# A pool-mixer trunk on one core: three products of its second input phase as seven inner products in place, the output weights formed and split only behind them

## The chip, the cores and the metric

The kernel runs on one core of one Trainium2 chip. The metric is the device time of one execution in microseconds (us); smaller is better. Executions of this kernel before the change took 909.81 to 910.54 us.

## The reference

With DEPTH = 1 only the pooling mixer runs: a row norm, an input projection to 2 x 1024 channels (values `u` and a gate), trailing means over 2, 4, 8 or 16 frames minus the value itself in four groups of 256 channels, a 256 x 256 map for each group, bias, scale, SiLU gate, an output projection, the residual sum and a last row norm. x is 4096 rows of 1024 float32.

```python
normed = rms_norm(h, norm_w[i])
u, gate = jnp.split(normed @ in_w, 2, axis=-1)
ug = u.reshape(b, s, POOL_GROUPS, POOL_GROUP_DIM)
pooled = jnp.stack([trailing_mean(ug[:, :, g], w) for g, w in enumerate(POOL_WINDOWS)], axis=2) - ug
mixed = jnp.einsum('bsgc,gcd->bsgd', pooled, group_w) + group_b
y = mixed.reshape(b, s, POOL_WIDTH) * scale * jax.nn.silu(gate)
h = h + y @ out_w
return rms_norm(h, final_norm_w)
```

## The kernel before, in words

The group maps are folded into the value half of the input weights at the start. All large products are then done by Winograd's form of Strassen's scheme: a product of 2 x 2 blocks in seven block products P1 to P7 with sums and differences around them. Every operand is split into two float32r parts (`split`: ScalarE copies the high part, VectorE subtracts it from the operand for the low part), and a block product is three passes of matmuls (`mm3`, L603).

Three phases follow each other in the list `steps`: "a" and "b" (the first and the second half of the input projection's columns, NB = 4 blocks of 1024 rows each) and "o" (the output projection, 8 blocks of 512 rows). A step is one block product. In "a" and "b" the order is `ORDER_IN` = P1, P2, P7, P6, P5, P4, P3, and a step is 48 matmuls of 128x512 (`product_in`): four PSUM banks, in each two halves h of the contraction, two k, three passes. P1, P2, P7, P4 use banks 0 to 3 ("x" and "v"), P6, P5, P3 banks 4 to 7 ("y"), into which P1 is copied first (`evict_in`). P5 is added onto y after P6 has been copied out of it. In the later steps of phase "o", one P2 product is itself done with seven inner products (`product_inner`, L701), of 128x256 matmuls.

What lies around a step: `advance("load", ...)` loads operands three steps ahead, `advance("split", ...)` splits the operand of the next step into the four tiles `ops`, two of them for a step, `form(n + 2)` forms the sums two steps ahead, `pool_due` issues the pooling of an earlier block half, `run(n)` the product and its eviction. Behind `run`, `make_wo` (at P5 of blocks 1 and 2 of phase "b") loads a quarter pair of the output weights, scales it in place (`scale_rows`, L246), forms Winograd's sums (`combine`, four VectorE instructions of 128x1024) and stores them to the DRAM tiles `wod`; in block 3, `load_w` (after every step) loads one product's weights from `wod` and splits them into `w`.

SBUF tiles of 4 KB a partition come from two lists, `st` (NS = 11) and `vt` (NV = 8). `take` hands out the tile that was given back longest ago; whoever writes it waits for its last users, a DMA store included.

The order of the instructions on each engine is fixed when the kernel is built: the framework plays the program through with its own durations and lets each engine take, of what is ready, what the program names first. So an instruction can stand ahead of others that the program names before it, when those were not ready. `tc.issue_after(x)` keeps the instructions of its block, where they are on the engine of x, behind x.

Of the kernel before, what the change touches and what calls it, by code (L numbers as in the profile page):

```python
# [15 lines left out]
P = 128  # L16
# [48 lines left out]
def kernel(  # L65
# [54 lines left out]

    def renew(t):
        i = next(i for i, u in enumerate(sts) if u is t)
        return mem.tile([P, D], F32R, tag=f"st{i}", name=f"inner{i}")

    st.renew = renew
    vt = Slots(
        [mem.tile([P, 2 * (HIST + H)], F32, tag=f"vt{i}", name=f"vt{i}") for i in range(NV)]
    )
# [23 lines left out]
    def give(ap):  # L152
        next(p for p in (st, vt, early, early5) if id(ap) in p.used).give(ap)
# [343 lines left out]


    xs = [{} for _ in range(NB)]
    turn = [0]  # L500

    def next_op(pattern, **sizes):
        t = ops[turn[0] % 4]
        turn[0] += 1
        return t.rearrange(pattern, **sizes)

    first_saves = []

    def split_halves(us, saved=None):
        ts = []  # L510
        for h, u in enumerate(us):
            t = next_op("p (s a b) -> p s a b", s=2, a=2)
            split(t, u)
# [33 lines left out]
    def form_in(q, b, i):  # L547

        s = xs[b]
        if i in (P1, P2):  # L550
            if q == 0:
                for u in s["11" if i == P1 else "12"]:
                    normalize(b, 0, u)
        elif i == P7:
            if q == 0:
                for h in range(2):
                    normalize(b, 1, s["21"][h])
                    sub(s["21"][h], s["11"][h], s["21"][h])
        elif i == P6:
            s["2"] = [take(pool=early if (q, b) == (0, 0) else None) for _ in range(2)]  # L560
            for h in range(2):
                if q == 0:
                    normalize(b, 1, s["22"][h])
                sub(s["2"][h], s["22"][h], s["21"][h])
            for u in s.pop("21"):
                give(u)
            if q == 0:
                give(rstd.pop(b))
        elif i == P5:
            for h in range(2):  # L570
                add(s["11"][h], s["2"][h], s["11"][h])
            if (q, b) != (0, 0):
                for u in s.pop("2"):
                    give(u)

    def split_in(q, b, i):
        s = xs[b]
        key = {P1: "11", P2: "12", P6: "2", P7: "21", P5: "11", P4: "22", P3: "12"}[i]
# [11 lines left out]
    stores = []  # L590

    def form_s4(b):
        for u, s2 in zip(xs[b]["12"], xs[b]["2"]):
# [49 lines left out]
    def form_inner(stage):  # L643
# [13 lines left out]
                give(u)  # L657
            return
        r = inner_w["sums"][stage - 1]
        hi, lo = (kept.pop().rearrange(pattern, **sizes) for _ in range(2))  # L660
        copy(hi, r)
        sub(lo, r, hi.bitcast(F32))
        give(r)
# [480 lines left out]
    def run(n, between=None, behind=None, seeds=4):  # L1144
        kind, b, i = steps[n]
        sets = sets_of(kind, b)
        if kind == "o":
            product_out(i, split_up.pop(n), sets, n == len(steps) - 1)
            evict_o(b, i, sets)
        else:  # L1150
            product_in(i, split_up.pop(n), sets, i == P1, between, behind)
            evict_in(b, 0 if kind == "a" else 1, i, sets, seeds)

    pending = []

    def pool_later(n):
        kind, b, i = steps[n]
# [202 lines left out]

    scales, summed = {}, []
    stages = (P6, P5, P4)
    stages = (P6, P5, P4)

    for n in range(2, len(steps)):
        kind, b, i = steps[n]
# [55 lines left out]
        if kind in ("a", "b"):  # L1422
            pool_later(n)
            if kind == "a":
                pool_due(n)
            if kind == "b" and b == NB - 1:
                load_w(wod, i)
            if kind == "b" and b in (1, 2) and i == P5:
                make_wo(b - 1)
            if kind == "b" and b == NB - 1 and i == P3:  # L1430
                f = take("p (a b) -> p a b", a=2)
                nc.sync.dma_start(
                    out=f.rearrange("p a b -> p (a b)"), in_=final_w.partition_broadcast(P)
                )
                fw.append(f)
# [52 lines left out]
```

## Time and profile before

| | |
|---|---|
| median of 3 executions | 910.12 us (909.81 to 910.54) |
| profiled execution: time, span | 910.49 us, 908.7 us |
| granted TensorE clock | 0.999 |
| TensorE busy | 900.7 us, 99% of the span, 4320 matmuls |
| VectorE, ScalarE, GpSimd busy | 715.5, 485.9, 84.6 us |
| steps of phase "b", block 1: P1, P2, P7, P6, P5 begin at about | 397, 407.5, 417.9, 428.2, 438.6 us |

A step is 10.36 us long. The profile gives, for a group of instructions, the line, the engine, output<-input tiles, the shape, the count, then busy us and the mean ns of one, then the idle time of the engine ahead of them and what ended it. The difference of 1.8 us between time and span lies outside the span and is taken as unchanged.

### The profile page before, as it was taken

To read this page: it belongs to the slowest core of one execution; us is meant where nothing else is said; L and a number is where in the kernel's file an instruction comes from. 1 tells how busy PE (TensorE), PEld (TensorE's weight loads), DVE (VectorE), ACT (ScalarE), POOL (GpSimd) and SP (SyncE) were. 2 spreads that over 40 slices of the span, in tenths; PEclk is the share of its full clock that TensorE was granted. 3 is DMA by queue.
4 is the path that set the end of the run, shared out by engine and by line. 5 is a ranking of instruction groups with operands and counts; after the bars stand their busy time and mean duration, and the time that the engine had idled before them with its cause. 6 is when DMAs were issued, how large, how long until landed. Compare 5 with 4: busy or idle time off the path is not lost.

```text
span 908.7 us, 11590 instructions
## 1 busy us (share of the span) xinstructions
PE 900.7 (99%) x4320; PEld 790.1 (87%) x4320; DVE 715.5 (79%) x843; ACT 485.9 (53%) x735; POOL 84.6 (9%) x166
## 2 busy tenths in 40 slices
PE   9999999999999999999999999999999999999997
PEld 7888888888888888888888888888888898988886
DVE  3889995985995997685786599599759768868686
ACT  7869547447446555355345445645545535445444
POOL 0020100100110000000000000001122113212200
PEclk9999999999999999999999999999999999999999
DMA  9987776577575454134616715618585675675732
GB/s 343 401 300 230 268 241 240 190 267 245 218 271 193 162 207 140 47 140 138 255 72 217 267 70 174 200 54 225 179 234 160 169 205 162 163 220 156 180 139 94
DMA packets 70841, 178.10 MB, mean 196 GB/s; under 512 B 6528, under 2 KB 24320, under 8 KB 70784
## 3 DMA queue, kind: packets, MB, share of 16 engines
q1 hardware_dynamic: 58160, 144.82, 46.0%
q0 software_dynamic: 11904, 31.48, 13.3%
q10 hardware_dynamic: 720, 1.06, 0.3%
q8 instruction: 34, 0.56, 0.3%
q14 instruction: 23, 0.19, 0.1%
HBM read 116.50 MB, written 60.83 MB: 195 GB/s over the span
## 4 chain that ended last, share of the span: by engine, by line
PE 95%; DVE 2%; DMA 1%; ACT 1%; issue 0%; DVEq 0%; ACTq 0%; SPq 0%
PE bank L603 89%; PE bank L701 3%; PE bank L406 3%; DMA st<-wvd 1%; DMA t3d<-st 0%; DMA early<-in_group_w 0%; DVE vt L1067 0%; DVE st L159 0%; ACT st L974 0%; ACT st L446 0%; DVE vt L162 0%; PE bank L472 0%; DVE op L159 0%; DVE vt L1026 0%; DVE st L156 0%
## 5 line engine op out<-in xcount | busy, mean ns | idle before, releaser
L603 PE MATMUL bank<-op,w 128*128 128x512 f32 x2688 | 581.2, 379 | 0.2 <-ACT st L165 0.2
L603 PEld LDWEIGHTS bank<-op,w 128*128 128x128 f32 x2688 | 507.8, 189 | 72.9 <-ACT st L165 0.6
L603 PE MATMUL bank<-w,op 128*128 128x512 f32 (+1 forms) x1212 | 262.2, 377 | 0.0
L603 PEld LDWEIGHTS bank<-w,op 128*128 128x128 f32 x1212 | 226.0, 189 | 31.0
L159 DVE TENSOR_TENSOR op<-st,op 128x1024 fp32r<-128x1024 f32 x129 | 156.5, 1220 | 76.4 <-ACT op L165 76.0
L165 ACT ACTIVATE op<-st 128x1024 fp32r<-128x1024 f32 x129 | 134.7, 1052 | 123.3 <-PE bank L603 82.6
L165 ACT ACTIVATE vt<-bank 128x512 f32<-128x512 f32 x105 | 61.4, 593 | 44.7 <-PE bank L603 44.2
L159 DVE TENSOR_TENSOR op<-vt,op 128x1024 fp32r<-128x1024 f32 x43 | 52.4, 1220 | 20.8 <-ACT op L165 20.6
L165 ACT ACTIVATE op<-vt 128x1024 fp32r<-128x1024 f32 x43 | 45.0, 1052 | 28.9 <-PE bank L603 24.9
L165 ACT ACTIVATE st<-bank 128x512 f32<-128x512 f32 x67 | 39.0, 592 | 38.0 <-PE bank L603 26.1
L884 POOL DMA_DIRECT2D st<-in_x x19 | 16.9, 894 | 387.7 <-DVE op L159 354.1
L159 DVE TENSOR_TENSOR st<-st,st 128x1024 f32<-128x1024 f32 (+1 forms) x43 | 46.7, 1108 | 3.2 <-ACT st L943 1.3
L165 ACT ACTIVATE bank<-bank 128x512 f32<-128x512 f32 x48 | 27.9, 581 | 35.6 <-PE bank L603 35.4
L755 DVE TENSOR_TENSOR_SCAN vt<-vt,window 128x1040 f32<-128x1040 f32 x16 | 38.1, 2379 | 2.8 <-ACT vt L165 2.7
L159 DVE TENSOR_TENSOR w<-st,w 128x1024 fp32r<-128x1024 f32 x25 | 30.2, 1220 | 11.7 <-ACT w L165 11.7
L165 ACT ACTIVATE w<-st 128x1024 fp32r<-128x1024 f32 x25 | 26.0, 1052 | 16.3 <-PE bank L603 10.8
L806 DVE SCALAR_TENSOR_TENSOR st<-vt,colt,st 128x512 f32<-128x512 f32 x46 | 32.4, 746 | 1.7 <-ACT st L165 1.6
L165 ACT ACTIVATE st<-st 128x1024 f32<-128x1024 f32 x16 | 16.9, 1058 | 29.9 <-DVE st L156 29.7
L801 DVE SCALAR_TENSOR_TENSOR vt<-vt,vt 128x1024 f32<-128x1024 f32 x24 | 29.3, 1221 | 0.3
L947 DVE SCALAR_TENSOR_TENSOR vt<-vt,ors,st 128x1024 f32<-128x1024 f32 x18 | 22.5, 1282 | 8.0 <-POOL ors L225 8.0
L162 DVE TENSOR_TENSOR st<-st,vt 128x1024 f32<-128x1024 f32 x22 | 26.1, 1216 | 2.1 <-DMA vt<-rd 2.1
L1067 DVE TENSOR_TENSOR st<-bank,st 128x512 f32<-128x512 f32 x23 | 15.8, 689 | 13.8 <-PE bank L603 13.7
(136 smaller groups left out, 661.6 us busy)
## 6 DMA issues: line engine op xcount, KB each, us to landing
st<-in_xt SPq DMA_DIRECT2D x28, 512.0 KB, 5.9
sd<-st POOLq DMA_DIRECT2D x28, 512.0 KB, 4.3
st<-sd SPq DMA_DIRECT2D x24, 512.0 KB, 4.4
yd<-st SPq DMA_DIRECT2D x23, 512.0 KB, 2.6
st<-in_x SPq DMA_DIRECT2D x20, 512.0 KB, 6.3
st<-yd SPq DMA_DIRECT2D x20, 512.0 KB, 4.7
out<-vt SPq DMA_DIRECT2D x18, 512.0 KB, 4.5
st<-wod SPq DMA_DIRECT2D x15, 512.0 KB, 3.4
```

The source lines that it names most:

```text
L159: return nc.vector.tensor_tensor(out=dst, in0=a, in1=b, op=ALU.subtract)
L162: nc.vector.tensor_tensor(out=dst, in0=a, in1=b, op=ALU.mult)
L165: return nc.scalar.activation(dst, src, func)
L406: latest[0] = nc.tensor.matmul(ps, a[:, kk, 2 * j + t, :], maps, start=t + m == 0, stop=t == 1 and m == len(pairs) - 1,).ins
L603: latest[0] = nc.tensor.matmul(ps, a, b, start=start and n == 0, stop=stop and n == 2, skip_group_check=True).ins
L701: latest[0] = nc.tensor.matmul(ps, x1, x2, start=i in (P1, P7) and k + n == 0, stop=k == 1 and n == 2, skip_group_check=True,).ins
L755: nc.vector.tensor_tensor_scan(out=sums_[:, HIST:], data0=flat[:, HIST:], data1=flat[:, HIST - win : 2 * end - win], initial=first_sum, op ...
L801: nc.vector.scalar_tensor_tensor(out=s[:, :, at : at + H], in0=s[:, :, at : at + H], scalar=1.0 / win, in1=v[:, :, HIST:], op0=ALU.mult, o ...
L806: nc.vector.scalar_tensor_tensor(out=sg[:, j], in0=s[:, j, at : at + H], scalar=bias_c[2 * grp + j], in1=sg[:, j], op0=ALU.add, op1=ALU.mult,)
L884: nc.gpsimd.dma_start(out=hs[b][half, j][:, n], in_=x[row_of(b, half, j), n * H : (n + 1) * H], accum_op=ALU.add,)
L947: nc.vector.scalar_tensor_tensor(out=us[j], in0=us[j], scalar=rs[:, j : j + 1], in1=fw[0], op0=ALU.mult, op1=ALU.mult,)
L1067: partial["added"] = nc.vector.tensor_tensor(out=dst, in0=src, in1=dst, op=ALU.add).ins
```

## The change

In blocks 1 to 3 of phase "b" the step P7 is no longer `product_in` but `product_seven`. Its block product is cut once more into 2 x 2 cells and done by seven inner products, each twelve matmuls of 128x256. The four cells lie in place, in the four banks v: cells 1 and 3 in the two halves of v[0] and v[1], cells 0 and 2 in those of v[2] and v[3] ("mirrored"). Partial results go from cell to cell by ScalarE copies (`move`), one by way of an SBUF tile (`held`), and two VectorE additions end the step. The operand is not split twice but four times (`split_seven`: two tiles of sums and the two plain halves), into all four tiles of `ops`. The next step's operand, for P6, is split inside the product (`middle`, `end`).

The inner weights are formed in block 0 (`form_seven`): three tiles of `st` are kept for them until P7 of block 3, and the others lie in the place of the P7 weights. `make_wo` goes from behind P5 to behind P7 of blocks 1 and 2, and its ScalarE and VectorE instructions have to stay behind the last copy and the last addition of P7 (`ends`). In block 3 nothing is loaded after P1 and P2; after P7 the output weights of P1, after P6 those of P2 and P7, after P5 those of P6 and P5, all behind `ends`. `form_s4` goes from the split of P6 to the end of P7.

```diff
+    def split_seven(s):
+        us = s["21"]
...
+        front, back = (take("p (n k s a) -> p n k s a", n=2, k=2, s=2) for _ in range(2))
+        sub(back[:, 0], a11, a21)
+        sub(back[:, 1], a22, back[:, 0])
+        add(front[:, 0], back[:, 1], a11)
+        sub(front[:, 1], a12, back[:, 1])
...
+        sums(front, (P5, P3))
+        plain_op(0, {P1: 0})
+        def second():
+            sums(back, (P7, P6))
+        def third():
+            plain_op(1, {P2: 0, P4: 1})
+            for u in s.pop("21"):
+                give(u)
+            ops[:] = [ops[n] for n in (1, 2, 0, 3)]
...
+    def form_seven(stage):
...
+            for _ in range(3):
+                places_in.append(next_kept())
+                kept_in.append(st.keep())
...
+    def product_seven(t, v, middle, end):
+        def cell(n, c):
+            return v[2 * (1 - n % 2) + c][:, n // 2 * 256 : (n // 2 + 1) * 256]
+        def into(i, n):
+            for c in range(2):
+                cs = slice(c * P, (c + 1) * P)
+                for k in range(2):
...
+                    for m, (x1, x2) in enumerate(((a[0], b[0]), (a[0], b[1]), (a[1], b[0]))):
+                        latest[0] = nc.tensor.matmul(
+                            cell(n, c).rearrange("p (a s) -> p a s", s=2), x1, x2,
+                            start=i == P1 and k + m == 0, stop=k == 1 and m == 2,
+                            skip_group_check=True,
+                        ).ins
+        def move(dst, src):
+            for c in range(2):
+                done = copy(cell(dst, c), cell(src, c))
+            return done
+        held = take()
+        into(P1, 1)
+        into(P5, 3)
+        with tc.issue_after(move(0, 1).ins):
+            middle()
+            for c in range(2):
+                copy(held[:, c, 0:256], cell(3, c))
+        into(P6, 1)
+        into(P2, 0)
+        move(2, 1)
+        into(P7, 2)
+        into(P3, 1)
+        moved = move(3, 2)
+        into(P4, 2)
+        with tc.issue_after(moved.ins):
+            end()
+        for c in range(2):
+            bank = v[c].rearrange("p (j b) -> p j b", j=2)
+            added = nc.vector.tensor_tensor(
+                out=bank, in0=bank, in1=held[:, c, 0:256].unsqueeze(1).to_broadcast([P, 2, 256]),
+                op=ALU.add,
+            )
+        give(held)
+        return moved.ins, added.ins
...
+            if inner_in(q, b, i):
+                us, parts = xs[b]["2"], []
+                at["split"] += 1
+                def next_half():
+                    parts.append(split_half(us[len(parts)]))
+                ends[:] = product_seven(split_up.pop(n), sets["v"], next_half, next_half)
+                if b == NB - 1:
+                    give_kept(*places_in)
+                split_up[n + 1] = parts
+            else:
+                product_in(i, split_up.pop(n), sets, i == P1, between, behind)
+            if "second" in seven:
+                seven.pop("second")()
+            evict_in(b, q, i, sets, seeds)
+            if "third" in seven:
+                seven.pop("third")()
...
     def split_reach(kind, b, i):
+        if kind == "b" and b > 0 and i == P6:
+            return 0
...
+        if kind == "b" and b == 0 and i in forming_seven:
+            with tc.issue_after(latest_split[0]), tc.issue_after(latest_copy[0]):
+                form_seven(forming_seven.index(i))
...
             if kind == "b" and b == NB - 1:
-                load_w(wod, i)
-            if kind == "b" and b in (1, 2) and i == P5:
-                make_wo(b - 1)
+                with tc.issue_after(ends[0]), tc.issue_after(ends[1]):
+                    for j in {P1: (), P2: (), P7: (P1,), P6: (P2, P7), P5: (P6, P5)}.get(i, (i,)):
+                        load_w(wod, j)
+            if kind == "b" and b in (1, 2) and i == P7:
+                with tc.issue_after(ends[0]), tc.issue_after(ends[1]):
+                    make_wo(b - 1)
```

More of the change, by code (lines that the diff above doesn't have):

```diff
@@ L122, in renew, with give_kept, next_kept @@
         i = next(i for i, u in enumerate(sts) if u is t)
-        return mem.tile([P, D], F32R, tag=f"st{i}", name=f"inner{i}")
+        return mem.tile([P, 2, H], F32R, tag=f"st{i}", name=f"inner{i}")
     st.renew = renew
+    def give_kept(*places):
+        for i in places:
+            sts[i] = mem.tile([P, D], F32, tag=f"st{i}", name=f"st{i}")
+            Slots.clock += 1
+            st.free.append((Slots.clock, sts[i]))
+    def next_kept():
+        return next(i for i, u in enumerate(sts) if u is st.free[0][1])
     vt = Slots(
@@ L564, in form_in @@
                 sub(s["2"][h], s["22"][h], s["21"][h])
-            for u in s.pop("21"):
-                give(u)
+            if not inner_in(q, b, P7):
+                for u in s.pop("21"):
+                    give(u)
             if q == 0:
@@ L659, in form_inner @@
         r = inner_w["sums"][stage - 1]
-        hi, lo = (kept.pop().rearrange(pattern, **sizes) for _ in range(2))
+        hi, lo = (
+            kept.pop().rearrange("p x (y s a) -> p x y s a", y=2, s=2) for _ in range(2)
+        )
         copy(hi, r)
@@ L1150, in run @@
         else:
[L1151 to L1154 removed]
+            q = 0 if kind == "a" else 1
+            if inner_in(q, b, i):
+                us, parts = xs[b]["2"], []
[6 more added lines that the diff above has]
+                split_up[n + 1] = parts
+            else:
+                product_in(i, split_up.pop(n), sets, i == P1, between, behind)
[4 more added lines that the diff above has]
+                seven.pop("third")()
+            if inner_in(q, b, i):
+                form_s4(b)
+                for u in xs[b].pop("2"):
+                    give(u)
+    pending, ends = [], []
     def pool_later(n):
```

75 lines of the change are left out of this document (68 added, 7 removed).

## The prediction

> **What bounds the kernel now.** I read the page first, then who waited for whom on TensorE, then the chain that ended last.
>
> ```profile
> span 908.7 us, 11590 instructions
> PE 900.7 (99%) x4320; PEld 790.1 (87%) x4320; DVE 715.5 (79%) x843; ACT 485.9 (53%) x735; POOL 84.6 (9%) x166
> PE 95%; DVE 2%; DMA 1%; ACT 1%; issue 0%; DVEq 0%; ACTq 0%; SPq 0%
> ...
> PE bank L1175 <- PEq L1473: 0.8, 1, 0.8
> PE bank L406 <- DMA early<-in_group_w: 0.4, 1, 0.4
> PE bank L603 <- ACT st L165: 0.2, 1, 0.2
> ...
> 702.93 3.35 PE bank L701 x30
> ...
> 712.80 25.90 PE bank L603 x120
> ```
>
> The matmuls are the span: 900.7 of 908.7 us, and all waits of TensorE together are 1.4 us. So a matmul saved is time saved, and a wait that is new is time lost, with nothing to take it back. The last two rows give both prices. A 128x512 matmul takes 25.90/120 = 0.2158 us, a 128x256 one 3.35/30 = 0.1117 us, a little over half.
>
> **Term 1, the matmuls.** A P7 step is 48 x 0.2158 = 10.36 us. Its successor is 7 x 12 = 84 matmuls of 128x256, 84 x 0.1117 = 9.38 us. That is 0.98 us a block, 2.94 us in three blocks, and all that the change can bring. The count should go from 4320 to 4320 + 3 x 36 = 4428.
>
> **Term 2, waits inside the new P7.** Between the inner products stand copies from cell to cell, so TensorE now depends on ScalarE in the middle of a step. I need the delays.
>
> ```profile
> L603 PEld LDWEIGHTS bank<-op,w 128*128 128x128 f32 x2688 | 507.8, 189 | 72.9 <-ACT st L165 0.6 <-ACT bank L165 0.4
> L159 DVE TENSOR_TENSOR op<-st,op 128x1024 fp32r<-128x1024 f32 x129 | 156.5, 1220 | 76.4 <-ACT op L165 76.0
> L165 ACT ACTIVATE op<-st 128x1024 fp32r<-128x1024 f32 x129 | 134.7, 1052 | 123.3 <-PE bank L603 82.6 <-DVE st L159 11.0 <-PE bank L701 7.9
> L165 ACT ACTIVATE st<-bank 128x512 f32<-128x512 f32 x67 | 39.0, 592 | 38.0 <-PE bank L603 26.1 <-DVE vt L159 4.8 <-DVE st L159 3.7
> L165 ACT ACTIVATE bank<-bank 128x512 f32<-128x512 f32 x48 | 27.9, 581 | 35.6 <-PE bank L603 35.4
> ...
> 220.27 0.61 ACT st L165
> 220.88 0.04 issue
> 220.92 1.13 PE bank L603 x4
> ...
> 417.00 1.89 PE L603 MATMUL bank<-op,w 128*128 128x512 f32 x8
> 418.07 0.60 ACT L165 ACTIVATE vt<-bank 128x512 f32<-128x512 f32 x1 [0.70 <-PE bank L603]
> 418.56 1.99 ACT L165 ACTIVATE op<-st 128x1024 fp32r<-128x1024 f32 x2
> 419.64 2.36 DVE L159 TENSOR_TENSOR op<-st,op 128x1024 fp32r<-128x1024 f32 x2 [4.45 <-ACT op L165]
> ```
>
> This is the seam between P2 and P7 of block 1. Eight matmuls start from 417.00 every 0.216 us; the fourth starts at 417.65, takes 0.38 and ends at 418.03, and the last eviction of P2 starts at 418.07. P7 therefore begins at 417.87, which I call T = 0, and ScalarE can start 0.20 us after TensorE has gone on. The way back costs 0.04 us and a weight load of 0.19, together 0.23, taken as 0.25. A copy of 256 columns is an estimate from the rows: (1052 - 592)/512 = 0.90 ns a column, so 581 - 256 x 0.90 = 351 ns. An inner product takes 12 x 0.1117 = 1.34 us, 0.67 for each of its two banks.
>
> No row here has one engine at one half of a bank while TensorE writes the other, so the wait has two ends. If a copy waits for the matmuls of its own cell alone, every `move` has an inner product of 1.34 us beside it (P5, P2, P3), against 0.20 + 2 x 0.35 + 0.25 = 1.15 us: nothing is lost, the lower end is 0. A gain is excluded, as the matmuls are counted already. If it waits for all of its bank, then move(0, 1) has to wait for P5, which writes the other half of v[0] and v[1], and P6 has to wait until both that move and the copies into `held` have read them. I follow this in T. P5 leaves its two banks at 2.01 and 2.68; the move's copies run 2.21 to 2.56 and 2.88 to 3.23. Next on ScalarE is the split of `middle` (1.05) to 4.28, then `held`, done for v[0] at 4.60. P6 can start at 4.85 instead of 2.68. In this gap the builder can put P2, which writes v[2], v[3], once `third` is split: the eviction of P2's last bank ends at 0.80, the copy at 1.85, the subtraction at 3.12, so P2 starts at 3.37. That leaves 0.69 us idle ahead of P2, 0.14 ahead of P6, and 0.13 each ahead of P7 and P4, whose moves reach only 0.13 beyond what runs beside them: 1.09 us. If TensorE keeps the order of the program, P6 ahead of P2, the same sums give 2.17 + 0.13 + 0.13 = 2.43.
>
> I take 1.09: evictions such as that at 418.07 stand behind the last matmul of their whole bank, and the builder does draw work forward on other engines, as term 3 shows. Three blocks: 3.27 us, between 0 and 7.29. So the inner products by themselves are worth about nothing.
>
> [...]
>
> **Term 3, what now stands ahead of P5.** `make_wo` starts behind `ends`, and P6, P5 follow at once.
>
> ```profile
> 412.71 1.34 ACT L246 ACTIVATE st<-st,colt 128x512 f32<-128x512 f32 x2 [3.46 <-DMA st<-in_out_w]
> ...
> 430.92 1.93 ACT L246 ACTIVATE st<-st,colt 128x512 f32<-128x512 f32 x3
> ...
> L246 ACT ACTIVATE st<-st,colt 128x512 f32<-128x512 f32 x12 | 8.1, 715 | 5.1 <-DMA st<-in_out_w 5.0
> ...
> 432.89 1.23 DVE L159 TENSOR_TENSOR st<-st,st 128x1024 f32<-128x1024 f32 x1 [0.61 <-ACT st L246]
> ...
> 436.55 1.22 DVE L159 TENSOR_TENSOR op<-st,op 128x1024 fp32r<-128x1024 f32 x1
> 437.80 1.22 DVE L159 TENSOR_TENSOR st<-st,st 128x1024 f32<-128x1024 f32 x1
> ...
> 553.66 1.05 ACT L165 ACTIVATE w<-st 128x1024 fp32r<-128x1024 f32 x1
> 554.61 1.03 ACT L165 ACTIVATE op<-st 128x1024 fp32r<-128x1024 f32 x1
> ...
> st<-in_out_w SPq DMA_DIRECT2D x6, 512.0 KB, 4.0
> wod<-st SPq DMA_DIRECT2D x10, 512.0 KB, 2.7
> ```
>
> Today `make_wo(0)`, named behind P5 (which ends at about 449), is drawn forward: its scalings run from 412.71 to 432.85, wherever ScalarE is idle, its sums from 432.89 to 439. The two rows at 553 and 554 show the rule that decides when two are ready: the weight split, named behind P1, goes ahead of the operand split named in the next step. In the new kernel `make_wo` is named behind P7, hence ahead of P5's split, which belongs to step P6, and cannot start before T = 9.55, the end of the last move. From there ScalarE has P6's second half (0.94 from start to start, by the pair at 418.56), four evictions of P7 (0.49, 418.07 to 418.56), eight scalings (0.62, by the pair at 412.71) and only then P5's first half: 9.55 + 0.94 + 1.96 + 4.96 = 17.4, its copy done at 18.5. The last tile to be loaded for `make_wo` is that of `held`, free at 10.3, landed at about 14.5, early enough to keep this queue closed. On VectorE the four sums begin at 17.45, 1.14 apart (the pair at 419.64), and stand ahead of P5's subtraction, which ends at 17.45 + 4.56 + 1.22 = 23.2. P5 can start at 23.45; it is due at 9.38 + 1.09 + 10.36 = 20.83. TensorE waits 2.6 us, in blocks 1 and 2: 5.2 us.
>
> A second chain ends at the same place in block 1. Three kept tiles leave 16 of 19, and when P7 has run 6 are free, of which `make_wo` takes 5; counting gives and takes, both tiles into which P6 is evicted are then those of its first and third quarter. The first is written at 19.8 and stored (2.7) at 22.5; the eviction of y[0] ends at 23.1, again 2.5 us late. The lower end of the term is 0, if the builder's clock lets P5's split in ahead of the scalings; 1.5 each if the subtraction gets in between the sums, as that at 436.55 does today. The upper end is 2.6 here and 2 us more for both, should a load land late. I take 2.6.
>
> **Term 4, block 3.** The tile for the pooling of block 2's second half is now that of `front`, so this pooling, 10 us of VectorE work, goes from P1 into P2 and pushes the subtraction of `third` by some 0.7 us past 3.12. I take 0.7, between 0 and 2.
>
> **What I cost at nothing, and its cover.**
>
> ```profile
> 407.60:418.00 10.40, 10.40 (x50) 9.11 (x49) 7.04 (x8) 4.79 (x8) 0.00 (x0) 1.00 0.39 145
> 418.00:428.40 10.40, 10.40 (x50) 9.11 (x49) 5.85 (x5) 6.52 (x9) 0.00 (x0) 1.00 0.37 114
> ...
> 563.00:573.40 10.40, 10.40 (x50) 9.11 (x49) 8.13 (x7) 7.16 (x10) 0.00 (x0) 1.00 0.40 115
> 573.40:583.80 10.40, 10.40 (x50) 9.11 (x49) 4.81 (x4) 6.21 (x9) 0.00 (x0) 1.00 0.76 247
> 583.80:594.10 10.30, 10.30 (x49) 9.01 (x49) 6.67 (x8) 4.89 (x8) 0.00 (x0) 1.00 0.49 150
> 594.10:604.50 10.40, 10.40 (x50) 9.11 (x49) 10.40 (x10) 4.34 (x6) 0.00 (x0) 1.00 0.16 50
> L159 DVE TENSOR_TENSOR vt<-vt,vt 128x512 f32<-128x512 f32 x2 | 1.3, 688 | 0.0
> ```
>
> In these stretches the third busy column is VectorE, the fourth ScalarE. The four sums of `split_seven` (4 x 0.69) and two more splits (2 x 1.22) are 5.2 us of VectorE, most of it in P2 and early P7, where 3.4 and 4.6 us are free. ScalarE gets 2.1 for the splits and 8 copies of 0.35. In block 3 the splits for output products P1 and P2 (4.9 us of VectorE) move behind P7, where 2.3 + 5.6 + 3.6 us are free before VectorE is full from 594 on. Without that cover, up to 2 us would come back in P4 or P3. Forming the inner weights in block 0 is eight subtractions and four copies over four steps, and nobody waits for them before block 1. Loads have three steps, 31 us, of lead.
>
> **The sum.** Against the profiled execution: 910.49 - 2.94 + 3.27 + 5.2 + 0.7 = 916.7 us. That execution is 0.37 above the median; against the median, 910.12 + 6.2 = 916.3 us.
>
> **The rivals.**
>
> Faster: copies wait by cell alone, or the builder fills the gaps, and P5's split comes in time. Its place is inside P7 and ahead of P5; it decides once waits are under 1.1 us in sum over all blocks. 910.12 - 2.94 = 907.2, up to 908.3. For it: each move does have 1.34 us of other matmuls beside it. Against: it needs ScalarE idle at three moments of each P7 and terms 2 and 3 both absent. Chance 0.22.
>
> No change: term 2 holds, term 3 does not, as `make_wo` has all of phase "b" left and could be drawn apart by late loads as today. 910.12 - 2.94 + 3.27 = 910.5, with term 4 911.2; 908.3 to 911.9. Chance 0.18.
>
> Slower by more: TensorE keeps the program's order in P7. 3 x 1.34 = 4.0 more, 920.3, with block 3 up to 922. Against: orders drawn forward elsewhere. Chance 0.15.
>
> My forecast, terms 1 to 4, 911.9 to 918.3: chance 0.45.
>
> **The numbers.** Runs of this kernel lie within 0.08%; 0.2%, 1.8 us, is about what a measurement can tell from no change, so faster is below 908.3, slower above 911.9. Faster 0.22, same 0.18, slower 0.60. The range takes in the faster case and the bulk of the last one: 907.2 to 921.0; about one in ten is left out. As both signs hold a share, the forecast's own range is 911.9 to 918.3.
>
> **What would show it.** Term 1: 252 matmuls of 128x256 on a new line, 30 in 3.35 us. Term 2: idle time of TensorE on that line in each of three steps, ended by ScalarE copies bank<-bank or st<-bank of 128x256, 1 us a block; none would bring the faster case, 2.4 the slower one. Term 3: a gap of 2 to 3 us at the start of P5 in blocks 1 and 2, ended by an op<-st subtraction or an eviction, with L246 closely packed ahead of it. If P5 starts on time while L246 is spread out, term 3 is wrong and the time is near 911. Term 4: a longer idle time in P7 of block 3 than in block 2.

## The result and the profile after

| | before | after |
|---|---|---|
| median, runs | 910.20 us (909.81 to 910.54, 5) | 919.86 us (917.46 to 920.67, 5) |
| ratio of the means | | 1.0103, 95% interval 1.0088 to 1.0118 |
| profiled execution, span | 910.49, 908.7 | 920.37, 918.6 |
| matmuls | 4320 | 4428 |

The change makes the kernel 1% slower. All ratios in this document are of means, while the times given are medians. 919.86 lies in the range that was given, 3.6 us above the predicted 916.3 and above the forecast's own range (to 918.3). These are the page of the changed kernel, its waits of TensorE (us in total, times, longest), and the two groups of the new matmuls:

```profile
span 918.6 us, 11909 instructions
PE 902.6 (98%) x4428; PEld 794.1 (86%) x4428; DVE 735.9 (80%) x875; ACT 497.0 (54%) x769; POOL 86.2 (9%) x166
PE 77%; DVE 11%; DMA 4%; issue 4%; ACT 3%; POOL 0%; SPq 0%; DVEq 0%; ACTq 0%; POOLq 0%
...
PE bank L709 <- ACT bank L175: 1.8, 1, 1.8
PE bank L756 <- DVE st L1222: 1.7, 1, 1.7
PE bank L856 <- DVE op L169: 1.2, 1, 1.2
PE bank L756 <- ACT bank L175: 1.2, 1, 1.2
PE bank L756 <- ACT st L175: 0.8, 1, 0.8
...
PE bank L709 <- DVE op L169: 0.4, 1, 0.4
PE bank L709 <- ACT vt L175: 0.3, 1, 0.3
...
L709 PE MATMUL bank<-op,w 128*128 128x256 f32 x144 | 19.0, 286 | 2.5 <-ACT bank L175 1.8 <-DVE op L169 0.4 <-ACT vt L175 0.3
...
L709 PE MATMUL bank<-op,inner 128*128 128x256 f32 x108 | 14.6, 293 | 0.0
```

Before, TensorE held 95% of the chain that ended last; now it holds 77%. The 252 matmuls are there, and the count is as worked out. Each wait is a single event, so it has a place and can be counted.

For a budget I took the start of every matmul from 400 us on. Time to the next start beyond its own pace (0.2158 us for 512 columns, 0.1117 for 256) is idle, and gaps above 0.05 us are summed. The kernel before has none there. Where the clock is halved (0.52, below), each matmul comes later than its pace, and the count takes this in as idle time too. Block 1 goes to 460 us, block 2 to 540, block 3 to 625, then the output phase.

| profiled run | block 1 | block 2 | block 3 | output | sum | median, us |
|---|---|---|---|---|---|---|
| before | 0 | 0 | 0 | 0 | 0 | 910.20 |
| after | 1.82 | 2.00 | 5.14 | 3.61 | 12.57 | 919.86 |

The saving of 2.94 and this idle time make +9.63. The two profiled executions differ by 9.88, so 0.25 us lie outside this count (smaller gaps, the time ahead of 400 us and behind the last matmul); the medians happen to differ by 9.66. The slowdown is waiting, with 1.6 us of halved clock behind one wait. Where it sits, each as the timeline has it (start, us, engine, what, count, idle before and what ended it). P7 of block 1, TensorE and then ScalarE:

```profile
417.60 4.55 PE L709 MATMUL bank<-op,w 128*128 128x256 f32 x36
421.98 0.64 PE L756 MATMUL bank<-op,w 128*128 128x512 f32 x2
422.45 2.95 PE L709 MATMUL bank<-op,inner 128*128 128x256 f32 x24
...
418.29 1.05 ACT L175 ACTIVATE op<-st 128x1024 fp32r<-128x1024 f32 x1
419.87 0.37 ACT L175 ACTIVATE bank<-bank 128x256 f32<-128x256 f32 x1 [0.53 <-PE bank L709]
420.54 0.37 ACT L175 ACTIVATE bank<-bank 128x256 f32<-128x256 f32 x1 [0.30 <-PE bank L709]
...
421.77 0.64 ACT L175 ACTIVATE st<-bank 128x256 f32<-128x256 f32 x2
```

P1, P5 and P2 form one group of 36, so P2 was drawn ahead of P6, and two 128x512 matmuls of the next step fill the gap that was left. About 0.56 us is lost here, and the same in block 2. Then P5 of block 1, with the same place of block 2 behind it:

```profile
439.81 2.43 PE L756 MATMUL bank<-op,w 128*128 128x512 f32 x10 [0.80 <-ACT st L175]
...
429.98 5.02 ACT L256 ACTIVATE st<-st,colt 128x512 f32<-128x512 f32 x8
434.87 2.96 ACT L175 ACTIVATE op<-st 128x1024 fp32r<-128x1024 f32 x3
438.17 1.06 ACT L175 ACTIVATE op<-st 128x1024 fp32r<-128x1024 f32 x1 [0.34 <-PE bank L756]
439.16 1.09 ACT L175 ACTIVATE st<-bank 128x512 f32<-128x512 f32 x2
...
509.72 2.01 ACT L175 ACTIVATE op<-st 128x1024 fp32r<-128x1024 f32 x2
511.62 1.08 ACT L175 ACTIVATE vt<-bank 128x512 f32<-128x512 f32 x2
```

P5 writes the banks out of which P6 is evicted. In block 1 the first of these evictions comes at 439.16, four operand copies behind the scalings, and TensorE stands still until it is done. In block 2 it goes into another kind of tile and comes behind two, at 511.62; there is no gap. Next, P2 of block 2:

```profile
485.86 1.35 PE L756 MATMUL bank<-op,w 128*128 128x512 f32 x5 [1.17 <-ACT bank L175]
...
485.10 0.23 ACT L175 ACTIVATE vt<-tails 128x32 f32<-128x32 f32 x1 [3.24 <-DMA yd<-vt]
485.23 0.58 ACT L175 ACTIVATE bank<-bank 128x512 f32<-128x512 f32 x1
```

A copy of 32 columns, the 16 in front of a block for the pool, drawn forward by the builder, waits 3.24 us for a tile that a store still reads. The copy of P1's bank behind it in ScalarE's queue is late by that, and P2 waits for its bank. Ahead of these small copies ScalarE idled 16.5 us before the change and, by their group, 36.1 after it (the line of before stands first):

```profile
L165 ACT ACTIVATE vt<-tails 128x32 f32<-128x32 f32 x28 | 6.4, 228 | 16.5 <-DVE vt L159 8.4 <-DVE vt L755 2.4 <-DMA yd<-vt 1.6
L175 ACT ACTIVATE vt<-tails 128x32 f32<-128x32 f32 x28 | 6.3, 227 | 36.1 <-DVE vt L910 17.4 <-DVE vt L169 8.4 <-DMA yd<-vt 5.3
```

Then P7 of block 3, and two windows (us; busy time and count of PE, PEld, DVE, ACT, POOL; granted clock; DMA share; GB/s):

```profile
569.81 0.38 PE L709 MATMUL bank<-op,w 128*128 128x256 f32 x1 [1.82 <-ACT bank L175]
570.62 1.64 PE L709 MATMUL bank<-op,w 128*128 128x256 f32 x9 [0.44 <-DVE op L169]
...
564.39 1.18 ACT L175 ACTIVATE vt<-bank 128x512 f32<-128x512 f32 x2 [3.70 <-DVE vt L961]
567.22 0.35 ACT L175 ACTIVATE vt<-tails 128x32 f32<-128x32 f32 x2 [1.64 <-DVE vt L910]
...
554.25 1.23 DVE L169 TENSOR_TENSOR op<-vt,op 128x1024 fp32r<-128x1024 f32 x1 [7.35 <-ACT op L175]
555.51 2.39 DVE L910 TENSOR_TENSOR_SCAN vt<-vt,window 128x1040 f32<-128x1040 f32 x1
...
568.00:571.50 3.50, 1.25 (x8) 1.06 (x9) 3.50 (x5) 3.50 (x8) 0.00 (x0) 0.98 0.00 0
571.50:574.90 3.40, 3.40 (x17) 3.31 (x17) 3.40 (x4) 0.41 (x2) 0.00 (x0) 0.52 0.84 306
```

The scan of the pool can start only when `front` has been split (555.51). Evictions of P2 wait for a tile that the pool's last operation (L961) still uses, 3.70 us, a copy of 32 columns ahead of `third`'s split holds ScalarE, and TensorE waits. Behind the waits comes a second loss: for 3.4 us the granted clock is 0.52, half rate, and 17 matmuls take the time of some 30; by the count of idle time that is 1.6 us. Last, the output phase:

```profile
689.87 1.35 PE L756 MATMUL bank<-w,op 128*128 128x512 f32 x5 [1.75 <-DVE st L1222]
...
681.92 0.69 DVE L169 TENSOR_TENSOR vt<-st,vt 128x512 f32<-128x512 f32 x1 [11.20 <-DMA st<-wod]
```

VectorE waits 11.2 us for the second raw tile of the inner output weights, and the adds that free banks stand behind that wait in its queue. A second gap of 1.4 us, ahead of 712.97, is ended by an operand split on VectorE; what makes that split late is not shown.

### The profile page after: what moved, and what is told of

It is laid out like the page before. It is cut to its first block, busy times and chain, and to the rows that moved or that the text cites. A ratio compares the mean times of both kernels' runs of the same rounds, so it can differ in the third digit from the quotient of the medians.

```text
span 918.6 us, 11909 instructions
## 1 busy us (share of the span) xinstructions
PE 902.6 (98%) x4428; PEld 794.1 (86%) x4428; DVE 735.9 (80%) x875; ACT 497.0 (54%) x769; POOL 86.2 (9%) x166
## 4 chain that ended last, share of the span: by engine, by line
PE 77%; DVE 11%; DMA 4%; issue 4%; ACT 3%; POOL 0%; SPq 0%; DVEq 0%; ACTq 0%; POOLq 0%
PE bank L756 70%; PE bank L709 3%; PE bank L856 3%; DVE op L169 2%; DVE vt L910 2%; DMA st<-wod 1%; DMA vt<-yd 1%; PE bank L416 1%; DVE vt L956 1%; DVE st L169 1%; DMA early<-in_wut 1%; DVE st L166 1%; DVE w L169 1%; ACT w L175 1%; ACT op L175 1%
## 5 line engine op out<-in xcount | busy, mean ns | idle before, releaser
L756 PE MATMUL bank<-op,w 128*128 128x512 f32 x2544 | 552.1, 380 | 2.0 <-ACT bank L175 1.2
L756 PEld LDWEIGHTS bank<-op,w 128*128 128x128 f32 x2544 | 480.9, 189 | 70.6 <-ACT bank L175 2.2
L756 PE MATMUL bank<-w,op 128*128 128x512 f32 (+1 forms) x1212 | 262.5, 377 | 1.7 <-DVE st L1222 1.7
L756 PEld LDWEIGHTS bank<-w,op 128*128 128x128 f32 x1212 | 226.4, 190 | 32.6 <-DVE st L1222 2.1
L175 ACT ACTIVATE vt<-bank 128x512 f32<-128x512 f32 (+1 forms) x116 | 66.1, 592 | 48.7 <-PE bank L756 43.8
L175 ACT ACTIVATE bank<-bank 128x512 f32<-128x512 f32 (+1 forms) x66 | 34.3, 522 | 42.8 <-PE bank L756 28.9
L175 ACT ACTIVATE st<-bank 128x512 f32<-128x512 f32 (+1 forms) x62 | 34.6, 579 | 29.5 <-PE bank L756 15.1
L169 DVE TENSOR_TENSOR st<-st,st 128x1024 f32<-128x1024 f32 (+2 forms) x36 | 37.7, 1059 | 8.3 <-ACT st L256 5.6
L169 DVE TENSOR_TENSOR w<-st,w 128x1024 fp32r<-128x1024 f32 (+1 forms) x26 | 30.8, 1202 | 4.8 <-ACT w L175 3.4
L175 ACT ACTIVATE w<-st 128x1024 fp32r<-128x1024 f32 (+1 forms) x26 | 26.7, 1037 | 7.8 <-DMA st<-wod 6.3
L961 DVE SCALAR_TENSOR_TENSOR st<-vt,colt,st 128x512 f32<-128x512 f32 x36 | 25.5, 751 | 0.6 <-ACT st L175 0.5
L1039 POOL DMA_DIRECT2D vt<-in_x x22 | 19.7, 943 | 65.9 <-DVE vt L866 34.0
```

The lines of the kernel that those rows point to most:

```text
L169: return nc.vector.tensor_tensor(out=dst, in0=a, in1=b, op=ALU.subtract)
L175: return nc.scalar.activation(dst, src, func)
L756: latest[0] = nc.tensor.matmul(ps, a, b, start=start and n == 0, stop=stop and n == 2, skip_group_check=True).ins
L961: nc.vector.scalar_tensor_tensor(out=sg[:, j], in0=s[:, j, at : at + H], scalar=bias_c[2 * grp + j], in1=sg[:, j], op0=ALU.add, op1=ALU.mult,)
L1039: nc.gpsimd.dma_start(out=hs[b][half, j][:, n], in_=x[row_of(b, half, j), n * H : (n + 1) * H], accum_op=ALU.add,)
```

## The experiments

Medians stand beside their own runs of the kernel before (910.35 to 910.47). The budget of idle time of all of them:

| profiled run | block 1 | block 2 | block 3 | output | sum | median, us |
|---|---|---|---|---|---|---|
| e1_pool_tile | 3.05 | 1.98 | 0.56 | 0.27 | 5.86 | 913.19 |
| e2_raw_tiles | 2.34 | 2.01 | 3.52 | 5.91 | 13.78 | 921.00 |
| e3_wo_at_p5 | 2.01 | 0.56 | 5.11 | 1.74 | 9.42 | 916.33 |
| e4_heads_late | 12.61 | 4.96 | 5.62 | 3.99 | 27.18 | 934.68 |
| e5_heads_gpsimd | 1.71 | 1.35 | 3.51 | 1.14 | 7.71 | 918.50 |
| e6_wo_alone | 0.07 | 0 | 0 | 0.35 | 0.42 | 910.63 |
| e7_p2_behind_p6 | 1.95 | 2.21 | 3.93 | 0.25 | 8.34 | 915.70 |
| f1_tile_wo | 1.96 | 0.56 | 2.14 | 0.26 | 4.92 | 911.45 |
| f2_tile_wo_heads | 0.56 | 1.96 | 2.06 | 0.26 | 4.84 | 913.71 |
| f3_heads_vector | 0.56 | 2.12 | 2.05 | 0.36 | 5.09 | 912.95 |
| f4_heads_vector_alone | 1.64 | 1.16 | 3.51 | 2.12 | 8.43 | 916.33 |
| f5_s4_late | 0.56 | 0.56 | 0.57 | 0.58 | 2.27 | 909.99 |

A profiled run need not be the median one. That of e5 was its fastest, 915.24, that of e1 its slowest, 914.86; those of f1, f2 and f3 took 912.06, 914.30 and 914.14. Part of this has nothing to do with the change: the 200th matmul, long before the changed steps, starts at 41.4 us in the kernels before and after, at 42.7 in e1 and f3, and at 40.9 in f1.

### The pool's tile

```
-        keep[0] = 5 if kind == "b" and b == NB - 1 else 3
+        keep[0] = 5 if kind == "b" and b == NB - 1 and i not in (P1, P2) else 3
```

> Against the changed kernel's 919.86 us. Nothing is left out; in the last block of the second phase the pool's tile and its companions may be taken as early in steps P1 and P2 as in the other blocks (the reserve of three free tiles instead of five), so the pool no longer gets the tile that the formula for the seven products still reads. Theory (the tile): the 5.2 us that the last block's P7 lost, the half-clock stretch included, shrink to what blocks 1 and 2 lose there, about 0.55 each, so the time falls by about 4.5 to 915.4, and no product there runs at a granted clock of 0.52. Rival (the work: VectorE and ScalarE of the last block are too full with the scan, the weight splits and the seven sums, whatever the tile): less than 1 us of change, 919 to 920. Rival by the clock: the waits go but the half-rate stretch stays, about 2 us of gain, 918.

Measured 913.19 us, ratio to before 1.0029 (1.0018 to 1.0040). TensorE and VectorE of block 3:

```profile
567.01 4.55 PE L709 MATMUL bank<-op,w 128*128 128x256 f32 x36
...
545.70 2.38 DVE L910 TENSOR_TENSOR_SCAN vt<-vt,window 128x1040 f32<-128x1040 f32 x1
```

The scan starts at 545.70 and no longer at 555.51, and block 3's P7 is like the other two, with 36 matmuls in the same 4.55 us. So the pool's late tile was the cause of 4.6 us there, of which 1.6 are the half rate. The gain is 6.7, as the output phase lost its two gaps too (3.3 us), which the expectation did not have, while block 1 lost 1.2 more.

### The place of the output weights

In the changed kernel (e3), and, in the kernel before, the move alone (e6):

```
-            if kind == "b" and b in (1, 2) and i == P7:
+            if kind == "b" and b in (1, 2) and i == P5:
```
```
-            if kind == "b" and b in (1, 2) and i == P5:
+            if kind == "b" and b in (1, 2) and i == P7:
```

> Against the changed kernel's 919.86 us. Nothing is left out; the forming and splitting of the output weights goes back behind step P5 in blocks 1 and 2 (still behind the ends of the same stores), P7 stays in seven products. The prediction's third term: 2.6 us of waiting ahead of P5 in each of the two blocks goes, 914.7. Theory from the trace after: only block 1 waits there, 0.96 us and the refills behind it, and block 2 does not, so 918.7 at best. Rival: the scalings and splits are as much work behind P5 and hold P4 in place of P5: no change or up to 1 us slower, 919.5 to 921.

> Against the kernel before, 910.35 us. This is the kernel before with one line changed: the output weights are formed and split behind P7 and not behind P5; P7 stays in eight products. The prediction's third term, taken alone, has P5 of blocks 1 and 2 wait 2.6 us each: 915.5. Theory from the traces (the delay of 1.2 us that the changed kernel shows in block 1 belongs to this move, and block 2 has cover): 911.5. Rival (it is the tiles that the seven products take which made it late; with the tiles of before the move costs nothing): 910.35.

e3 took 916.33 us, ratio 1.0067 (1.0050 to 1.0085); e6 took 910.63, ratio 1.0002 (0.9993 to 1.0011). In e6 nothing holds the step behind `ends`, and the builder drew it forward: block 1's scalings run from 398.86 to 420.11, most of them before P7. So e6 shows that the earlier place costs nothing in the kernel before; it does not show what `ends` and what the tiles of the changed kernel add. In e3 the gap ahead of block 1's P5 went, but block 1 lost as much elsewhere:

```profile
408.91 0.23 ACT L175 ACTIVATE vt<-tails 128x32 f32<-128x32 f32 x1 [8.86 <-DVE vt L910]
```

Again a copy of 32 columns ahead of the copy of a bank, now with 1.35 us for TensorE in block 1's P2, which waits for that bank. The 3.5 us of gain are 1.4 in block 2 and 1.9 in the output phase, where no weight is formed. So the step's own wait was worth about 1.2, not 5.2. Moving it also changes which tiles are handed to whom; that this brought the rest is argued, not shown.

### The raw tile of the output phase

```
             if len(kept) == 4:
+                keep[0] = 0
                 load_inner()
```

> Against the changed kernel's 919.86 us. Nothing is left out; one line frees the reserve before the raw output weights of the inner products are loaded, so that the second raw tile is one that is free at once and not the one that a store of the last finish still reads. Theory (the raw tile): the load moves from 671.9 us to some 650, the first subtraction of the inner weights no longer waits for it, VectorE's 11.2 us of idle time ahead of 681.9 goes, and with it the two gaps of 1.9 and 1.3 us on TensorE in the output phase that stand behind it: about -3.2, 916.7. Rival (VectorE's own amount of work in that phase): the gaps stay where they are or move, less than 1 us of change.

Measured 921.00 us, ratio 1.0113 (1.0096 to 1.0131). My theory falls. The raw tile came in time, but the next load took the late tile instead, and VectorE waited for that one:

```profile
683.12 1.22 DVE L169 TENSOR_TENSOR vt<-st,st 128x1024 f32<-128x1024 f32 x1 [8.14 <-DMA st<-yd]
...
689.20:692.60 3.40, 3.40 (x9) 2.70 (x8) 3.40 (x5) 0.45 (x1) 0.00 (x0) 0.50 0.03 7
...
571.60:575.00 3.40, 3.40 (x31) 3.33 (x31) 3.40 (x4) 0.83 (x3) 0.00 (x0) 1.00 0.83 308
```

The second row, a window, shows that part of the 5.91 us that e2 lost in its output phase is half rate: behind a gap of 2.2 us on TensorE nine matmuls take the time of some sixteen, 1.65 us. The third row is a by-product. Block 3 had the same waits (TensorE busy 1.24 of the 3.5 us ahead), yet the 3.4 us behind them ran at a granted clock of 1.00, with 31 matmuls and not 17. Its block 3 lost 3.52 us and not 5.14: the half-rate stretch there costs 1.6.

### ScalarE's queue behind the small copies

Held behind the last eviction (e4); by GpSimd in the second phase (e5); by VectorE (f4):

```
-                copy(v[:, :, 0:HIST], tails[:, g])
+                with tc.issue_after(evicted[0]):
+                    copy(v[:, :, 0:HIST], tails[:, g])
```
```
+                if q == 1:
+                    nc.gpsimd.tensor_copy(out=v[:, :, 0:HIST], in_=tails[:, g])
+                else:
+                    copy(v[:, :, 0:HIST], tails[:, g])
```
```
+                    nc.vector.tensor_copy(out=v[:, :, 0:HIST], in_=tails[:, g])
```

> Against the changed kernel's 919.86 us. Nothing is left out; the pool's copies of the 16 columns in front of a block, which the builder's order had drawn forward on ScalarE by some 65 us, are held behind the last eviction issued. Theory (a copy that waits for a tile blocks ScalarE's queue): the 3.2 us wait of ScalarE at 485 us goes, and with it the 1.4 us gap in block 2's P2; in block 3's P7 the same kind of copy stands ahead of an eviction, up to 1.6 more: 916.9 to 918.5. Rival: P2 in block 2 waits for the bank in any case, because the evictions of the step before are late: less than 0.5 us of change. Against it: the sums of the pool start later by the wait for the eviction, and the hand-over at the end of a block may be later, up to 1 us slower.

> Against the changed kernel's 919.86 us. Nothing is left out; in the second phase GpSimd, which has no work there, makes the pool's copies of the 16 columns in front of a block, in place of ScalarE, at the same place in the program. Theory (ScalarE's queue, in order, stood behind a copy that waited for a tile): ScalarE's waits ahead of these copies go, with them the 1.4 us ahead of block 2's P2 and part of block 3's P7 (up to 1.6), and the sums of the pool start no later than now: 917 to 918.5. Rival (the tile itself is late, whoever copies): the sums wait as long as before, but the seed copies are no longer behind them, so P2 gains and only block 3's P7 stays: 918.5. Rival (P2's bank is late for another reason): under 0.5 us of change. As in the run in which the copies were held back, more than 1 us slower if GpSimd's copy comes later than ScalarE's.

> Against the changed kernel's 919.86 us. Nothing is left out; the copies of the 16 columns by VectorE alone, without the other two edits. Theory: the gap of 1.4 us ahead of block 2's P2 goes and nothing takes its place (with GpSimd, whose copy took 0.9 to 1.1 us in the mean and up to 2.2, a wait of 1.0 inside block 2's P7 did): 918.3. The loss in block 3's P7 stays, as it hangs on the tile: not under 917. Rival (P7's waits inside come from VectorE's amount of work): as with GpSimd, 918.5, with the wait inside block 2's P7.

e4 took 934.68 us, ratio 1.0261 (1.0243 to 1.0278), far from any expectation. The pool started later, gave its tiles back later, and P2's evictions, which go into them, held P7 in all three blocks by 3.3 us. That is 9.8 of the 27.2 us. By my count of idle time 6.5 more are half rate behind gaps; the granted clock was 0.991 over this run, 0.998 to 0.999 in its runs of before. P7 of block 1, its 36 matmuls in 6.03 us and not 4.55:

```profile
421.07 6.03 PE L709 MATMUL bank<-op,w 128*128 128x256 f32 x36 [3.11 <-ACT vt L175]
```

e5 took 918.50 (1.0080, 1.0061 to 1.0099), f4 916.33 (1.0065, 1.0051 to 1.0078). In both the gap ahead of block 2's P2 is gone, so it did come from ScalarE's queue. In both a wait of 0.9 to 1.0 us inside block 2's P7 took its place, against f4's theory. f4 is below what I expected for two other reasons: its block 3 loses 3.51 and not 5.14, since the waits there, as long as before, were not followed by a half-rate stretch (its 108 matmuls with `inner` took 281 ns in the mean, as in e1, against 293 in the changed kernel), and its output phase loses 1.5 less. One copy took 1135 ns on GpSimd (e5) against 227 on ScalarE (the changed kernel) and 0.17 to 0.18 us on VectorE (f3); the times of e5 (915.24 to 919.08) and f4 (915.31 to 917.49) overlap all the same.

```profile
L943 POOL COPY vt<-tails 128x32 f32<-128x32 f32 x14 | 15.8, 1135 | 317.9 <-DVE vt L910 200.3 <-ACT tails L175 111.0 <-DMA yd<-vt 4.3
```

### The order inside P7

On top of the two edits of f1 below:

```
         into(P6, 1)
-        into(P2, 0)
+        with tc.issue_after(latest[0]):
+            into(P2, 0)
```

> Against the run with the pool's tile early and the output weights behind P5 (911.45 us), where each P7 of seven products loses some 0.55 us and its P2 runs ahead of its P6. Nothing is left out; one line holds the matmuls of P2 behind those of P6, as the program writes them. The second term of the prediction by its upper bound (the matmuls wait for the copies by bank, 2.43 us a block against 0.55): three times 1.9 more, 917. By its lower bound (they wait by cell): no change, 911.4. By the builder's order alone (P6 then waits for the sums that are split for it, which P2's 12 matmuls of 0.112 us hid): three times 0.7 to 1.3, 913.5 to 915.5.

Measured 915.70 us, ratio 1.0059 (1.0043 to 1.0074), 4.25 above f1, 1.42 a block. Block 1 (L757 is L756 moved by a line):

```profile
417.36 2.84 PE L709 MATMUL bank<-op,w 128*128 128x256 f32 x24
421.67 0.70 PE L757 MATMUL bank<-op,w 128*128 128x512 f32 x2 [1.48 <-ACT op L175]
422.21 1.50 PE L709 MATMUL bank<-op,inner 128*128 128x256 f32 x12
```

P6 starts 4.85 us after P7, just where the prediction's wait by bank had it, in this order and in the other. By the count of idle time each P7 loses 1.94 us and not 0.56, of which 1.64 are one gap. Drawing P2 forward is worth 1.4 us a block.

### Together

f1 has the edits of e1 and e3; f2 adds GpSimd's copies, f3 VectorE's; f5 is f3 with `form_s4` held back:

```
             if inner_in(q, b, i):
-                form_s4(b)
+                with tc.issue_after(seven_split[0]):
+                    form_s4(b)
```

`seven_split[0]` is the split that `third` makes; another line keeps it there.

> Nothing is left out; the pool's tile taken early in the last block, and the output weights formed and split behind P5 as before the change. The two edits alone gave 913.19 (-6.7 against the changed kernel's 919.86) and 916.33 (-3.5). If the two act at different places: 913.2 less the 1.3 and 0.4 us of block 1's P5 and the 1.3 of block 2's P2, plus about 0.9 for the longer gap in block 1's P1 that the second edit showed: 911.1. If the two overlap in the output phase (both were rid of its gap of 1.9 us): 912 to 913. Before is at 910.35.

> Nothing is left out; the pool's tile early in the last block, the output weights behind P5, and GpSimd copying the pool's 16 columns in the second phase. If ScalarE's queue behind these copies is what is left over: 910.35 for the kernel before, less 2.94 us of matmuls, plus 0.55 in each P7: about 909.1, and up to 910.3 with the small gaps of the output phase. Rival: the gap ahead of block 1's P2 stays because its tile is late: 910.5 to 911.5.

> Against the run with the pool's tile early and the output weights behind P5 (911.45 us, before 910.40). Nothing is left out; on top of those two edits the pool's copies of the 16 columns in the second phase are made by VectorE, whose own scan of the tile before is what they wait for, and no longer by ScalarE. Theory (ScalarE's in-order queue behind these copies makes the two gaps that are left, 1.35 us in block 1's P1 and 1.30 in block 3's P1, and VectorE waits for nothing there that it would not wait for anyway): 911.45 - 2.65 = 908.8, faster than before by 1.6; 14 copies of about 0.1 us are VectorE's price. Rival (with these gaps gone the next work is late, as when GpSimd made the copies: 1.8 us in the P7 of blocks 2 and 3): 911 to 913.

> Against the run with the pool's tile early, the output weights behind P5 and VectorE copying the pool's 16 columns (912.95 us; before 910.47). Nothing is left out; on top of those three edits the two subtractions that form the operand of step P3 (form_s4, 128x1024, 1.22 us each, not needed for four more steps) are held behind the split of the second half of P7's own rows, ahead of which VectorE's queue had them. Theory (what keeps the change from paying is VectorE's queue in front of P7: the splits for its P2 end 1.67 and 1.60 us late in blocks 2 and 3): the splits end 2.3 us earlier, both waits shrink to the 0.25 of block 1, 912.95 - 2.8 = 910.2, no measurable difference from before, down to 909.1 (before less 2.94 for the matmuls plus 0.55 for each P7) if nothing else is late. Rival (ScalarE's copies for these splits, behind P2's evictions, are late by themselves): 912 to 913. Rival (the next late thing, P6's operands or the add of the held cells, takes the place): 911 to 912.

f1 took 911.45 us (1.0010, 1.0001 to 1.0019), f2 913.71 (1.0036, 1.0024 to 1.0049), f3 912.95 (1.0030, 1.0019 to 1.0042). In f1 two gaps are left in P2 of blocks 1 and 3, both behind small copies in ScalarE's queue. (The expectation of f3 puts them in P1; by the number of matmuls up to P7 they lie 6 and 12 matmuls into P2.) f2 and f3 are rid of them and gain nothing: blocks 2 and 3 now lose 1.4 to 1.6 us more inside P7. The three budgets lie within 0.25 us. That the medians of f2 and f3 are 2.3 and 1.5 us above that of f1 is not explained by them: of the 2.1 us between the profiled runs of f1 and f3, 1.8 lie ahead of the 200th matmul, and by its budget f1 would take 912.4, so its other runs must have lost less than the profiled one; where, no profile shows. Here is f3 in block 2, TensorE and then VectorE:

```profile
495.47 1.49 PE L709 MATMUL bank<-op,w 128*128 128x256 f32 x11 [1.55 <-DVE op L169]
...
490.79 1.22 DVE L169 TENSOR_TENSOR st<-st,st 128x1024 f32<-128x1024 f32 x1
491.93 1.22 DVE L169 TENSOR_TENSOR st<-st,vt 128x1024 f32<-128x1024 f32 x1
493.06 1.22 DVE L169 TENSOR_TENSOR op<-vt,op 128x1024 fp32r<-128x1024 f32 x1
494.20 1.22 DVE L169 TENSOR_TENSOR op<-st,op 128x1024 fp32r<-128x1024 f32 x1
```

P2 waits for the split that ends at 495.42. Ahead of it are the two subtractions of `form_s4` (490.79, 491.93), whose result is needed four steps later. Held back in f5:

```profile
489.28 4.55 PE L710 MATMUL bank<-op,w 128*128 128x256 f32 x36
...
491.06 1.22 DVE L169 TENSOR_TENSOR op<-st,op 128x1024 fp32r<-128x1024 f32 x1 [0.71 <-ACT op L175]
```

The split ends 3.0 us after P7's first matmul and no longer 4.6, the 36 matmuls are one group again, and every block loses 0.56. f5 took 909.99 us against 910.38: ratio 0.9999, 0.9990 to 1.0008. With every other wait repaired, the seven products are worth no measurable time. By the budget, 2.94 saved less 1.69 inside P7 and 0.58 in the output phase would leave 0.67 us, which is less than these runs can tell apart.

## Why the prediction was right in sign and short in size

**Term 1, matmuls, -2.94: right.** 4428 matmuls, and the saving with the idle time gives the difference of the profiled executions to 0.25 us.

**Term 2, waits inside P7, 1.09 a block: mechanism right, size 0.56.** In T (0 at 417.60) the move's copies start at 2.27 and 2.94 (predicted 2.21 and 2.88), and P6 at 4.85 (4.85). The first copy starts at 419.87, when P5's last matmul of that bank has ended, though its own cell was written 1.3 us earlier. The copy in this program thus waits for all of its bank; what an unguarded access would do, no run shows. Two steps were mis-sized. P2's first matmul multiplies the high parts and needs only the copy, so 25 matmuls run before the first wait, of 0.25 and not 0.69. And the builder put two matmuls of the next step into the 0.14 ahead of P6. The rival "slower by more" had a right price, 4.0 for the other order against 4.25 in e7, but that order was not taken.

**Term 3, P5 waits 2.6 in blocks 1 and 2: wrong in size, and half of the mechanism with it.** The packed scalings are there: eight from T = 12.38 to 17.4 (predicted 12.45 to 17.41). The step that failed is "the four sums ... stand ahead of P5's subtraction": VectorE took that subtraction behind the first sum, from T = 18.57 to 19.79. The prediction had priced "in between the sums" at 1.5 each, which fits a place behind the third; behind the first its own steps give 17.45 + 1.14 + 1.22 = 19.8, before P5 is due at 20.83, and so no wait. With that, block 2 waits not at all. Block 1 waits 0.96 us, ended by an eviction of P6's banks, at the place that the second chain named. Loss 1.2 and not 5.2. In e6 the earlier place costs nothing, with the tiles of before and nothing held behind `ends`; which of the two matters, no run separates.

**Term 4, block 3's P7, 0.7: right cause, a seventh of the size.** It measured 4.6 (5.14 less 0.56). That the pool would go from P1 into P2 was in the prediction, and its scan did begin ten microseconds later than in e1. But I counted only one subtraction that it pushes. All that waits for its tiles came after it: P2's evictions, ScalarE's queue, TensorE, and then the clock. e1 shows the cause, e2 the share of the clock.

**Not in the sum.** 1.4 us in P2 of block 2, from a copy of 32 columns in ScalarE's queue; f4 and e5 show the cause. 3.6 in the output phase. And "cost at nothing" held for ScalarE's and VectorE's totals, but not for their order: what f2 and f3 gave back came from VectorE's queue ahead of P7. So the total came near by luck, since terms 2 and 3 were 5.6 us too high and term 4 and the missing ones 8.9 too low. It is luck too that the time lies in the whole range: the room above 918.3 was given for TensorE keeping the program's order in P7, which did not happen.

**Open.** The output phase's gaps went in e1, e7, f1, f2 and f3, where nothing near them was edited, and e2 only moved them. All these kernels hand the tiles on in another order; which handing-on decides was not tried. That the runs of the changed kernel spread over 3.2 us where those of before spread over 0.7 fits a half-rate stretch and a late load that come in some executions. The granted clocks agree, with 0.999 in the fastest run (917.46) and 0.996 in those of 919.86 and 920.67, but only profiled runs show where the time goes.

## What to carry to other kernels

Where the bound engine has no slack, a change that saves its work has to be read for what it does to tiles and queues: here one tile that the pool got late cost 4.6 us in one step, where 0.98 us was saved. Follow each tile that changes hands to whoever gets it next, and list what stands behind its first user in that engine's queue, however small that user is. When a wait is taken away and the time does not fall, look at the next engine's queue ahead of the same step: an operation that nobody needs soon may stand in front.

## What the hardware showed that I had not expected

A stall can have a second price, and it was not paid each time. In the changed kernel, after a stretch in which TensorE was busy 1.25 of 3.5 us (568.00 to 571.50), the granted clock was 0.52 for the next 3.4 us and 128x256 matmuls started 0.213 us apart in place of 0.112; with the same stall in e2 (1.24 of 3.5 us, 568.10 to 571.60) it stayed at 1.00. In e2's output phase it was 0.50 for 3.4 us from 689.20, behind the gap of 2.2 us, and in the changed kernel's it was 1.00 from 690 to 693, behind 2 us in which TensorE was busy for 0.25. What decides between the two is not shown; nothing was run to move a stall in time.

And in the changed kernel the first matmul behind a wait, 128x256 or 128x512, was followed by 0.10 us of idle time before its train went on (at 439.81 the next start came after 0.320 us in place of 0.2158, at 420.65 after 0.213 in place of 0.1117), so each wait inside P7 cost that much more.
